# Differences of cumulative sums in a state-space layer: a matmul with split bfloat16 sums in place of a broadcast load

## The chip, the core and the metric

The kernel runs on one core of a Trainium2 chip. Its time is the device time of one execution, in microseconds (us). The core has TensorE (PE in the profile: matmuls; PEld: the loading of their weights), VectorE (DVE), ScalarE (ACT) and GpSimd (POOL). SyncE's queue (SP) issues nearly all DMA transfers here. Each of these takes its instructions strictly in order. SBUF is the on-chip memory, and PSUM is the small memory that TensorE writes; this kernel uses it in tiles of one bank, [128, 512] float32.

## What is computed

One inference step of a two-layer network on 128 context tokens and 1024 latent tokens, 1152 in all, of width 1024. The even layer, where the change is, has a bidirectional state-space scan beside a pooling branch; the odd layer is attention. The scan works in 9 chunks of 128 tokens, with 16 heads in 4 groups. For each chunk and head it needs the decay between every two tokens of the chunk:

```
a = chunk(dt * A)
a_cs = jnp.cumsum(a, axis=2)
seg = a_cs_t[..., :, None] - a_cs_t[..., None, :]
l_mat = jnp.exp(jnp.where(lower, seg, NEG_INF))
cb = jnp.einsum('bclgn,bcsgn->bcgls', Cc, Bc)
y_diag = jnp.einsum('bcgrls,bcsgrp->bclgrp', cb[:, :, :, None] * l_mat, xdt)
```

There is one such scan forward and one backward over the same tokens, each with its own `dt` and `A`. `seg` is a 128 x 128 matrix of differences for each chunk, head and direction. On one side of the diagonal the forward difference is the smaller one, on the other side the backward one, so that the smaller of the two belongs to the direction that is wanted.

## The kernel before, in words

Matrix products run on pairs of float16 numbers, high and low part, as three matmuls each (`mm3`, L330 to L332). The order of PE is the order of the program. The other engines and SP are ordered by a scheduler of the framework that follows buffers, dependences and priorities. Tiles come from pools with a fixed number of buffers; a new tile waits until the last reader of the buffer's former tile is done.

The even layer is one long stage. `ssd_steps` (L741) goes through the four head groups. For a group it first runs seven **storing steps** of one direction's scan (L841 to L851), then nine **output steps** of the other direction (L868 to L911), one chunk each. Between the small matmuls of these steps the generator yields, and `ssd_group` (L710) fills in a measured amount of other matmuls (`F.take`): projections of later blocks, which are large and always ready. So PE alternates between a few scan matmuls, each waiting for what other engines prepare, and a stretch of this fill.

The small matmuls write PSUM tiles with tag `ss`, of which there are four (five late in the stage). In an output step these are `cb` in `prep` (L815), the state's product `st` (L770), the output `yd` (L889) and the carried states' part `yo` (L898). They take the banks in turn.

What the change touches:

- `dt_branch` (L570) computes the cumulative sums on PE: by token (`cs`, L617 to L623) and by head as rows (L641 to L648). Eight DMAs write the rows to DRAM as `csrow` (L650).
- `decay(c)` (L794) prepares the weights of one chunk in a tile `E` of [128, 2, 4, 128] float32 (halves 0 and 1, four heads), of which there are `NE = 5` buffers. It loads the rows of both directions, copied to all 128 partitions, in one 512 KB DMA (L798). Then for each of four heads: ACT adds the token's own sum to half 0 (L801), DVE adds it to half 1 and takes the smaller of both (L802), and ACT writes the `dt` weights over half 1 (L804). ACT's exponential over four heads (L806) and POOL's product of both halves (L807) end it.
- `prep(c)` (L812) multiplies the weights by `cb` on DVE (L825), and ACT and POOL split the result into M, high and low (L510, L511). Four heads' products of M with x make `yd` (L893).
- `decay` is called in three of the seven storing steps (L847) and at the start of six of the nine output steps, for the chunk three ahead (L870), which makes 36 calls; `prep` is called for the chunk two ahead (L872).

In the profile below, psss is any tile of tag `ss`, xs and xshl are the inputs of the state's product, hst, hb and hf the states, o and u the convolution's buffers, whl the projections' weights.

Of the kernel before, what the change touches and what calls it, by code (L numbers as in the profile page):

```python
# [10 lines left out]
F32 = mybir.dt.float32  # L11
F16 = mybir.dt.float16
I32 = mybir.dt.int32
# [19 lines left out]
# even layer: the projections between the scans, by group; the fill (us of the tensor engine) of a group and the  # L33
# shares of it before its first step, per stored state, in either half of an output step, and per context state; the
# steps of the storing scan after which M is prepared
# [9 lines left out]
# odd layer: the fill of the first block of a head's queries, behind the first head's projections; the first block of a  # L45
# window head against the others; the score banks
# [3 lines left out]
NE = 5  # L50
# atanh(z) / z = 1 + s (c0 + c1 s + ...), s = z**2 <= 1/9, to 4e-10
# [20 lines left out]
class Filler:  # L72
    """projections whose matmuls are laid between the attention's and the scans'"""
# [11 lines left out]
    def to_front(self):  # L85
        """the jobs added with front=True from here on come next, behind the one under way"""
        self.pos = 1 if self.begun else 0
# [40 lines left out]
class OutProj:  # L128
    """x_new = x + gate * (g @ w_out), 128 columns of the result at a time; with rby the first half of g is
    scaled by it (per token) on its way out of PSUM"""  # L130
# [21 lines left out]
    def part(self, nb, ps, c0, c1, i):  # L152
        """the i-th k-tile of the order"""
# [6 lines left out]
    def begin(self, n, nb=0):  # L160
        """up to the n-th k-tile of block nb, all chunks of tokens"""
        for i in range(self.k0[nb], n):
            for ps, (c0, c1) in zip(self.pss[nb], CH3):
                self.part(nb, ps, c0, c1, i)
        self.k0[nb] = n
# [20 lines left out]
    def run(self, xres, ssq, chunk_done, chunks, before=None):  # L186
        """the rest; chunk_done(x tiles, first, last token) once a chunk is whole"""
# [34 lines left out]
class Builder:  # L222
# [82 lines left out]
    # ---------------------------------------------------------------- weights  # L305
    def load_w(self, src, nk=KD, n=P, scale=None, rows=None, pool=None):
        """[128, nk, n] fp32 weights -> (hi, lo) fp16 of 64 * w (* a column scale, or one per k-tile)."""
# [19 lines left out]
    def mm3(self, out, ah, al, bh, bl, start, stop):  # L327
        """out (+)= (ah + al).T @ (bh + bl) without the product of the two low parts"""
# [5 lines left out]
    def g_proj(self, src, hs, evac, pre=None):  # L334
        """channel-major projection: evac(psum [128 ch, 384 tok], first, last token); pre: its weights, and the
        chunks that are done"""
# [16 lines left out]
    def tok_proj(self, src, hs, evac):  # L353
        """token-major projection: evac(psum [128 tok, 3, 128 ch], first chunk)"""
# [13 lines left out]
    # ---------------------------------------------------------------- norms  # L368
    def rsqrt(self, out, v, w, pool=None):
        """out = v**-0.5 elementwise for small [128, w] tiles, v > 0: a first guess from the bits, then Newton"""  # L370
# [11 lines left out]
    def rstd_stats(self, ssq, c0, c1, n):  # L382
        """ssq [128, T] (squares summed over the k-tiles) -> diagonal tiles of rstd for tokens c0:c1"""
# [35 lines left out]
    # ---------------------------------------------------------------- ada  # L419
# [13 lines left out]
    def ada(self, blocks, tag, tile, ahead=False):  # L433
        """up to four column blocks (layer, first column, width up to 512) of the modulations, on column tiles of the
        array; mods [128, 24, 2]: shift 0:8, scale 8:16 (+1), gate 16:24 (/64)"""
# [52 lines left out]
    def modulate(self, hs, xs, rb, mods, c0, c1, ks=range(KD)):  # L488
        """h = x * rstd * (1 + scale) + shift as fp16 (hi, lo) for tokens c0:c1"""
# [23 lines left out]
    # ---------------------------------------------------------------- prologue  # L513
    def prologue(self):
        """the first norm, 512 channels at a time, with the first two projections of the even layer"""
# [225 lines left out]
    def ssd_steps(self, g):  # L741
# [126 lines left out]
        for n, c in enumerate(order):  # L868
            if n + 3 < NCH:
                decay(order[n + 3])  # L870
# [773 lines left out]
```

## Time and profile before

| | |
|---|---|
| three runs | 2298.39, 2302.61, 2303.87 us; median 2302.61 us |
| the profiled execution | span 2299.9 us, from its first to its last instruction; no other time is given for it |
| busy PE, PEld | 2025.4 us (88%), 1449.5 us (63%) |
| busy DVE, ACT, POOL | 1658.4 us (72%), 1275.3 us (55%), 1070.7 us (47%) |
| DMA | 283.17 MB, mean 123 GB/s |
| the 36 broadcasts | 512.0 KB each, 4.0 us from issue to landing |

"Busy" counts time in which an instruction runs. PE's matmuls are pipelined, so that one of 384 columns lasts some 0.33 us but the next starts 0.16 us after it. PEclk is the mean clock that TensorE was granted, as a share of full speed. "A <- B" in the list of waits means that A stood idle until B was done.

### The profile page before, as it was taken

The numbers are of one execution on the slowest core, as the hardware profiler recorded it, in microseconds if no ns is written. First come the engines' busy times: TensorE is split into PE (matmuls) and PEld (weight loads), VectorE is DVE, ScalarE is ACT, GpSimd is POOL, SyncE is SP. The second block draws the span as 40 slices with busy tenths as digits, with TensorE's granted clock in tenths as the row PEclk, the third lists the DMA queues.
The fourth block names the chain that finished last, engine by engine and source line by source line (L and its number), as shares of the span: only waits on it lengthen the run. The fifth ranks groups of instructions, "written<-read, shape, count | busy, mean of one in ns | idle before, by whom it ended". The sixth has DMA issues, their size and how long they took to land. (4 is left out here: it accounts for less than half of the span.)

```text
span 2299.9 us, 51010 instructions
## 1 busy us (share of the span) xinstructions
PE 2025.4 (88%) x20258; PEld 1449.5 (63%) x20258; DVE 1658.4 (72%) x3483; ACT 1275.3 (55%) x3432; POOL 1070.7 (47%) x997
## 2 busy tenths in 40 slices
PE   5997788788999999989898898998978898988997
PEld 2654475654657555657586686676666777676566
DVE  5878989789585544768978978878888767663334
ACT  5575656666464211447666666676667756673321
POOL 1378677876774100154534435445446656552001
PEclk9998899998999999999999999999999999999999
DMA  7221514224657412136445455455466867889412
GB/s 283 63 82 53 152 46 122 78 82 132 224 180 209 172 63 85 63 100 121 98 109 123 90 121 121 89 122 110 96 121 137 162 145 152 168 170 206 147 47 83
DMA packets 434990, 283.17 MB, mean 123 GB/s; under 512 B 374432, under 2 KB 385216, under 8 KB 434752
## 3 DMA queue, kind: packets, MB, share of 16 engines
q1 hardware_dynamic: 433776, 279.34, 49.0%
q8 instruction: 158, 2.59, 0.5%
q10 hardware_dynamic: 976, 0.58, 0.1%
q14 instruction: 80, 0.66, 0.1%
HBM read 133.38 MB, written 29.05 MB: 71 GB/s over the span
## 5 line engine op out<-in xcount | busy, mean ns | idle before, releaser
L330 PE MATMUL psmm<-h,whl 128*128 128x384 f16 (+1 forms) x1104 | 366.4, 333 | 9.7 <-DVE V L1205 3.8
L331 PE MATMUL psmm<-h,whl 128*128 128x384 f16 (+1 forms) x1104 | 365.7, 332 | 2.4 <-DVE h L507 1.7
L332 PE MATMUL psmm<-h,whl 128*128 128x384 f16 (+1 forms) x1104 | 365.1, 332 | 0.0
L330 PE MATMUL psmm<-whl,h 128*128 128x128 f16 x1920 | 346.2, 225 | 0.0
L331 PE MATMUL psmm<-whl,h 128*128 128x128 f16 x1920 | 345.8, 224 | 0.0
L332 PE MATMUL psmm<-whl,h 128*128 128x128 f16 x1920 | 345.5, 224 | 0.0
L331 PEld LDWEIGHTS <-whl 128*128 128x128 f16 x2256 | 224.8, 100 | 155.4 <-issue 30.7
L332 PEld LDWEIGHTS <-whl 128*128 128x128 f16 x2256 | 224.4, 99 | 155.1 <-issue 16.0
L330 PEld LDWEIGHTS <-whl 128*128 128x128 f16 x2256 | 225.5, 100 | 149.4 <-issue 21.5
L1307 POOL TENSOR_TENSOR phl<-p,phl 128x1152 f16<-128x1152 f32 (+1 forms) x72 | 158.4, 2200 | 242.4 <-ACT phl L1306 208.7
L324 DVE SCALAR_TENSOR_TENSOR whl<-w,whl 128x512 f16<-128x512 f32 x248 | 211.3, 875 | 67.8 <-ACT whl L323 67.4
L330 PEld LDWEIGHTS <-h 128*128 128x128 f16 x2520 | 251.2, 100 | 9.5 <-issue 3.8
L331 PEld LDWEIGHTS <-h 128*128 128x128 f16 x2520 | 251.1, 100 | 7.6 <-issue 1.9
L332 PEld LDWEIGHTS <-h 128*128 128x128 f16 x2520 | 250.9, 100 | 0.0
L1289 ACT ACTIVATE p<-psS,sms 128x384 f32<-128x384 f32 (+1 forms) x240 | 136.4, 570 | 100.3 <-DVE sms L1286 100.2
L1387 POOL TENSOR_TENSOR phl<-p,phl 128x1024 f16<-128x1024 f32 (+2 forms) x72 | 134.2, 1864 | 120.4 <-ACT phl L1386 120.1
L323 ACT ACTIVATE whl<-w 128x512 f16<-128x512 f32 x248 | 140.0, 609 | 81.3 <-PE psmm L332 44.7
L1173 POOL TENSOR_TENSOR sw<-sw,sin 128x384 f32<-128x384 f32 (+1 forms) x78 | 84.7, 1087 | 147.7 <-DVE sw L1172 134.9
L1280 PEld LDWEIGHTS <-Q 128*128 128x128 f16 x800 | 73.7, 98 | 126.0 <-issue 91.3
L504 POOL TENSOR_TENSOR h<-mt,h 128x384 f16<-128x384 f32 (+2 forms) x32 | 29.3, 925 | 251.6 <-ACT h L503 251.6
L1280 PE MATMUL psS<-K,Q 128*128 128x384 f16 (+1 forms) x480 | 109.5, 323 | 41.6 <-ACT p L1289 41.4
L1303 DVE SCALAR_TENSOR_TENSOR p<-p,sms,p 128x384 f32<-128x384 f32 (+1 forms) x200 | 136.7, 718 | 2.0
(394 smaller groups left out, 6242.5 us busy)
## 6 DMA issues: line engine op xcount, KB each, us to landing
w<-in_wod SPq DMA_DIRECT2D x52, 512.0 KB, 3.7
w<-in_wev SPq DMA_DIRECT2D x40, 512.0 KB, 4.1
E<-csrow SPq DMA_DIRECT2D x36, 512.0 KB, 4.0
Q<-qhl SPq DMA_DIRECT2D x64, 288.0 KB, 4.5
go_dr<-gl SPq DMA_DIRECT2D x15, 576.0 KB, 3.2
wada<-in_w_ada SPq DMA_DIRECT2D x32, 256.0 KB, 5.8
o<-in_w_ada SPq DMA_DIRECT2D x16, 512.0 KB, 5.9
xT<-in_w_ada SPq DMA_DIRECT2D x16, 512.0 KB, 5.9
```

Of the source, the lines that this page charges most:

```text
L323: nc.scalar.activation(hl[:, 0, a:e], w[:, a:e], AF.Copy if scale is None else AF.Identity, scale=sc)
L324: nc.vector.scalar_tensor_tensor(hl[:, 1, a:e], w[:, a:e], sc, hl[:, 0, a:e], ALU.mult, ALU.subtract)
L330: mm(out, ah, bh, start=start, stop=False)
L331: mm(out, ah, bl, start=False, stop=False)
L332: mm(out, al, bh, start=False, stop=stop)
L504: nc.gpsimd.tensor_tensor(h[:, 1, a:b], o, h[:, 0, a:b], ALU.subtract)
L1173: nc.gpsimd.tensor_tensor(sw[:, o:], sw[:, o:], self.sinT[:, a:b], ALU.mult)
L1280: nc.tensor.matmul(sv, q[:, m, x, qs], k[:, m, o + c0:o + c1], start=x == 0, stop=x == 1)
L1289: nc.scalar.activation(pm[:, c0:c1], ss[j], AF.Exp, bias=nb, accum_out=sm[:, i:i + 1])
L1303: nc.vector.scalar_tensor_tensor(p[0][:, c0:c1], p[1][:, c0:c1], sm[:, 2:3], p[0][:, c0:c1], ALU.mult, ALU.add)
L1307: nc.gpsimd.tensor_tensor(phl[:, w:2 * w], p[0][:, :w], phl[:, :w], ALU.subtract)
L1387: nc.gpsimd.tensor_tensor(phl[:, 2 * w:4 * w], p, phl[:, :2 * w], ALU.subtract)
```

## The change

The sums `cs` are no longer added by token on ACT and DVE. Instead PE forms the difference. `dt_branch` splits each row of sums into three bfloat16 parts that add up to it (`part`, one ACT copy each and a DVE subtraction after the first two), and writes all three to DRAM. For each group six small DMAs (`load_csl`) put the parts of four heads and two directions on 24 partitions of a tile `csl`, whose partitions 24 to 26 hold -1. A tile `csr` has two slots; partitions 0 to 23 hold a constant pattern of ones (`pick`), and two small DMAs per chunk (`load_csr`) put the parts of that chunk's sums on partitions 24 to 26. One matmul for each direction then gives the differences of four heads in a whole bank of tag `ss`, with the sign turned round. ACT copies the first bank out, DVE takes the larger of it and the second, and the exponential turns the sign back.

```diff
-NE = 5
+NE = 4
...
+            part = self.tl(self.plp, [P, 2 * TW], BF16, "V", 3)[0:16]
...
-            for g in range(4):
-                nc.sync.dma_start(self.csrow[g, :, d].rearrange("c h l -> h c l"),
-                                  row[g * 4:(g + 1) * 4].rearrange("h (c l) -> h c l", l=P))
+            for i in range(3):
+                h = part[:, (i % 2) * TW:(i % 2) * TW + T]
+                nc.scalar.activation(h, row, AF.Copy)
+                if i < 2:
+                    nc.vector.tensor_tensor(row, row, h, ALU.subtract)
+                nc.sync.dma_start(self.csrow[d, i], h)
+        self.load_csl(0)
+        self.cs_seq = [(g, c) for g in range(4) for c in (range(NCH) if g % 2 == 0 else range(NCH - 1, -1, -1))]
+        self.load_csr(0)
+        self.load_csr(1)
+
+    def load_csl(self, g):
+
+        for d in range(2):
+            for i in range(3):
+                o = 12 * d + 4 * i
+                self.nc.sync.dma_start(self.csl[o:o + 4], self.csrow[d, i, g * 4:(g + 1) * 4])
+
+    def load_csr(self, n):
+
+        if n < len(self.cs_seq):
+            g, c = self.cs_seq[n]
+            for d in range(2):
+                self.nc.sync.dma_start(self.csr[24:27, n % 2, d].rearrange("i (h l) -> i h l", l=P),
+                                       self.csrow[d, :, g * 4:(g + 1) * 4, c * P:(c + 1) * P])
...
         def decay(c):
...
-            nc.sync.dma_start(ef, self.csrow[g, c].rearrange("d h l -> (d h l)").partition_broadcast(P))
+            pd = []
+            for d in range(2):
+                pd.append(self.pt("ss"))
+                nc.tensor.matmul(pd[d], self.csl[:, c * P:(c + 1) * P], self.csr[:, n % 2, d], start=True, stop=True)
+            self.load_csr(n + 2)
+            if g < 3 and n % NCH == NCH - 1:
+                self.load_csl(g + 1)
+            nc.scalar.activation(ef[:, :512], pd[0], AF.Copy)
+            nc.vector.tensor_tensor(ef[:, :512], pd[1], ef[:, :512], ALU.max)
             for hh in range(4):
                 i = g * 4 + hh
-                nc.scalar.activation(E[:, 0, hh], E[:, 0, hh], AF.Identity, bias=self.cs[:, c, i:i + 1])
-                nc.vector.scalar_tensor_tensor(E[:, 0, hh], E[:, 1, hh], self.cs[:, c, 16 + i:17 + i], E[:, 0, hh],
-                                               ALU.add, ALU.min)
                 nc.scalar.activation(E[:, 1, hh], self.tri[:, 0], AF.Identity, bias=self.dt[:, c, 16 + i:17 + i],
                                      scale=self.dtd[:, c, i:i + 1])
-            nc.scalar.activation(E[:, 0], E[:, 0], AF.Exp)
+            nc.scalar.activation(E[:, 0], E[:, 0], AF.Exp, scale=-1.0)
             nc.gpsimd.tensor_tensor(E[:, 0], E[:, 0], E[:, 1], ALU.mult)
...
         for n, c in enumerate(order):
-            if n + 3 < NCH:
-                decay(order[n + 3])
             if n + 2 < NCH:
                 Ms[order[n + 2]] = prep(order[n + 2])
...
                          xk[:, hh // 2, 1, c % 3, hc], True, True)
+            if n + 3 < NCH:
+                decay(order[n + 3])
             nc.vector.tensor_tensor(y[:, c], y[:, c], yd[:, :256], ALU.add)
```

The tile of `cs` is given up and lies in a shared buffer; `even` sets up `csl` and `csr` at its start, with three memsets and two copies on POOL and one load of `pick` on ACT's queue. The call in the output steps is moved behind the matmuls of `yd`.

The orders below show three places. The lines of the changed kernel are some 1 to 56 higher than those before; the numbers behind the names tell buffers and tiles apart.

PE, the first storing step of the first group. Before, behind the last matmul of the first state's product (psss_1390) comes fill at once (psada_1369):

```order
L332 LDWEIGHTS bk_149_1239
L332 MATMUL psss_1390<-xshl_1387,bk_149_1239 128x256
L330 LDWEIGHTS whl_1364
L330 MATMUL psada_1369<-h_309,whl_1364 128x384
L331 LDWEIGHTS whl_1364
L331 MATMUL psada_1369<-h_309,whl_1364 128x384
```

Now (the same product is psss_1419, the same fill psada_1398):

```order
L333 LDWEIGHTS bk_154_1268
L333 MATMUL psss_1419<-xshl_1416,bk_154_1268 128x256
L828 LDWEIGHTS csl_657
L828 MATMUL psss_1425<-csr_658,csl_657 128x512
L828 LDWEIGHTS csl_657
L828 MATMUL psss_1427<-csr_658,csl_657 128x512
L331 LDWEIGHTS whl_1393
L331 MATMUL psada_1398<-h_309,whl_1393 128x384
```

The two matmuls of the first `decay` now stand between the state's product and the fill, and with them what they read: `csl` and `csr`.

SP's queue, the same place. Before, writes of `csrow` (V_1196 and V_1216 are the two directions' rows), two transposing loads (bk), the first three broadcasts to E and a load of weights (w):

```order
L650 DMA csrow<-V_1196 4x9x128
L737 DMA_TRANSPOSE bk_151_1244<-bc_1045 128x6x128
L737 DMA_TRANSPOSE bk_149_1239<-bc_1045 128x6x128
L650 DMA csrow<-V_1196 4x9x128 x2
L650 DMA csrow<-V_1216 4x9x128 x2
L798 DMA E_1395<-csrow 128x1024
L798 DMA E_1515<-csrow 128x1024
L798 DMA E_1664<-csrow 128x1024
L313 DMA w_259_2039<-in_wev 128x1024
```

Now (V_1206 holds the parts of the first direction, V_1231 those of the second), behind the same transposing loads:

```order
L761 DMA_TRANSPOSE bk_156_1273<-bc_1054 128x6x128
L761 DMA_TRANSPOSE bk_154_1268<-bc_1054 128x6x128
L656 DMA csrow<-V_1206 16x1152 x2
L656 DMA csrow<-V_1231 16x1152
L667 DMA csl_657<-csrow 4x1152 x2
L656 DMA csrow<-V_1231 16x1152
L667 DMA csl_657<-csrow 4x1152
L674 DMA csr_658<-csrow 3x4x128
L656 DMA csrow<-V_1231 16x1152
L667 DMA csl_657<-csrow 4x1152
L674 DMA csr_658<-csrow 3x4x128
L314 DMA w_269_2049<-in_wev 128x1024
```

Writes of the parts and reads of what was written alternate in one queue, ahead of the next load of weights; one more read of `csl` and the next reads of `csr` follow behind it.

DVE, an output step of the second group, from the sums into y to the next xs. Before:

```order
L895 TENSOR_TENSOR y_3798<-y_3798,psss_4024 128x256
L904 TENSOR_TENSOR psss_4038<-psss_4038,ef_1182 128x512
L906 TENSOR_TENSOR y_3798<-y_3798,psss_4038 128x256 x2
L802 SCALAR_TENSOR_TENSOR E_4210<-E_4210,cs_1180 128x128 x2
L819 ISA dgs_4088,dgc_4087<-psss_4083,ident 128x128
L819 ISA dgc_4087 128x1
L802 SCALAR_TENSOR_TENSOR E_4210<-E_4210,cs_1180 128x128
L821 SCALAR_TENSOR_TENSOR dgc_4087<-dt_892,dgc_4087,rows 128x4
L825 TENSOR_TENSOR E_3960<-E_3960,psss_4083 128x512
L761 TENSOR_TENSOR x_564_4502<-xk_302_2356 128x256
L767 TENSOR_TENSOR xs_4506<-x_564_4502,dec_1189 128x256
```

Now:

```order
L927 TENSOR_TENSOR y_3821<-y_3821,psss_4030 128x256
L833 TENSOR_TENSOR E_4043<-psss_4046,E_4043 128x512
L936 TENSOR_TENSOR psss_4059<-psss_4059,ef_1191 128x512
L938 TENSOR_TENSOR y_3821<-y_3821,psss_4059 128x256 x2
L851 ISA dgs_4093,dgc_4092<-psss_4088,ident 128x128
L851 ISA dgc_4092 128x1
L857 TENSOR_TENSOR E_4043<-E_4043,psss_4088 128x512
L853 SCALAR_TENSOR_TENSOR dgc_4092<-dt_901,dgc_4092,rows 128x4
L785 TENSOR_TENSOR x_602_4504<-xk_319_2379 128x256
L791 TENSOR_TENSOR xs_4508<-x_602_4504,dec_1198 128x256
```

The four small instructions of L802 are gone, one of 512 elements (L833) stands in their place, and the product with `cb` (L857, before L825) now works on the same tile, E_4043, as L833 just ahead of it; before, E_4210 was prepared while the product worked on E_3960.

More of the change, by code (lines that the diff above doesn't have):

```diff
@@ L12 @@
 F16 = mybir.dt.float16
+BF16 = mybir.dt.bfloat16
 I32 = mybir.dt.int32
@@ L621, in dt_branch @@
                 nc.tensor.matmul(pc[:, o:o + 16], self.tri[:, d], a[:, o:o + 16], start=True, stop=True)
-        cs = t("cs")
+        cs = self.tl(self.plp, [P, TW], F32, "V", 3)[:, :n]
         nc.scalar.activation(cs, pc[:, :n], AF.Copy)
@@ L635, in dt_branch @@
         nc.vector.scalar_tensor_tensor(dec, dec, WS, dt, ALU.mult, ALU.mult)
-        self.dt, self.cs, self.ef, self.etot, self.dec = map(v3, (dt, cs, ef, etot, dec))
+        self.dt, self.ef, self.etot, self.dec = map(v3, (dt, ef, etot, dec))
         self.dtd = self.wt([P, NCH, 16], F32, tag="dtd", bufs=1)
         nc.vector.tensor_tensor(self.dtd, self.dt[:, :, 0:16], self.dt[:, :, 16:32], ALU.subtract)
-        self.csrow = self.dr.tile([4, NCH, 2, 4, P], F32, name="csrow")
+        self.csrow = self.dr.tile([2, 3, 16, T], BF16, name="csrow")
         for d in range(2):
             row = self.tl(self.plp, [P, TW], F32, "V", 3)[0:16, :T]
+            part = self.tl(self.plp, [P, 2 * TW], BF16, "V", 3)[0:16]
             for c0, c1 in CH3:
@@ L794, in decay @@
         def decay(c):
+            n = self.cs_n
+            assert self.cs_seq[n] == (g, c)
+            self.cs_n += 1
             ef = self.wt([P, 1024], F32, tag="E", bufs=NE)
             E = ef.rearrange("p (a b c) -> p a b c", a=2, b=4)
-            nc.sync.dma_start(ef, self.csrow[g, c].rearrange("d h l -> (d h l)").partition_broadcast(P))
+            pd = []
[7 more added lines that the diff above has]
+            nc.vector.tensor_tensor(ef[:, :512], pd[1], ef[:, :512], ALU.max)
             for hh in range(4):
                 i = g * 4 + hh
-                nc.scalar.activation(E[:, 0, hh], E[:, 0, hh], AF.Identity, bias=self.cs[:, c, i:i + 1])
-                nc.vector.scalar_tensor_tensor(E[:, 0, hh], E[:, 1, hh], self.cs[:, c, 16 + i:17 + i], E[:, 0, hh],
-                                               ALU.add, ALU.min)
                 nc.scalar.activation(E[:, 1, hh], self.tri[:, 0], AF.Identity, bias=self.dt[:, c, 16 + i:17 + i],
                                      scale=self.dtd[:, c, i:i + 1])
-            nc.scalar.activation(E[:, 0], E[:, 0], AF.Exp)
+            nc.scalar.activation(E[:, 0], E[:, 0], AF.Exp, scale=-1.0)
             nc.gpsimd.tensor_tensor(E[:, 0], E[:, 0], E[:, 1], ALU.mult)
@@ L1019, in even @@
         with self.scope("ssd"):
+            self.csl = self.wt([P, T], BF16, "csl", 1)
+            self.csr = self.wt([P, 2, 2, 512], BF16, "csr", 1)
+            self.cs_n = 0
+            nc.gpsimd.memset(self.csl, 0.0)
+            nc.gpsimd.memset(self.csr, 0.0)
+            nc.gpsimd.memset(self.csl[0:27], -1.0)
+            pick = self.tl(self.plp, [P, TW], F32, "V", 3)[0:24, :1024].rearrange("p (d a) -> p d a", d=2)
+            nc.scalar.dma_start(pick, A["pick"])
+            for i in range(2):
+                nc.gpsimd.tensor_copy(self.csr[0:24, i], pick)
             for kind, p in zip(("xa", "xb", "b", "c"), (*pre, None, None)):
@@ L1622, in layout @@
     L["rce"] = rce.reshape(-1)
+    pick = np.zeros((2, 3, 4, 2, 4, P), np.float32)
+    for d in range(2):
+        for h in range(4):
+            pick[d, :, h, d, h] = 1.0
+    L["pick"] = pick.reshape(24, 2, 512)
     return {k: np.ascontiguousarray(v) for k, v in L.items()}
```

## Prediction

> **What bounds the kernel now.** I read first the page, for the span of 2299.9 us, and then the table of stretches, because the change touches only the even layer's scans. The first and the last broadcast (L798) start at 131.6 and 671.4 us, so I cut 130 to 708 us into the four groups' storing and output steps. The columns are the stretch and its length, then busy us and count of instructions for PE, PEld, DVE, ACT and POOL, then PEclk, DMA share and GB/s:
>
> ```profile
> 130.00:182.00 52.00, 47.12 (x284) 28.24 (x283) 39.46 (x53) 35.71 (x90) 41.53 (x50) 0.93 0.23 79
> 182.00:277.00 95.00, 68.57 (x499) 42.74 (x498) 84.98 (x142) 56.88 (x137) 72.43 (x87) 0.86 0.33 97
> 277.00:333.00 56.00, 49.97 (x601) 40.20 (x600) 45.35 (x67) 33.03 (x91) 41.15 (x48) 1.00 0.31 92
> 333.00:414.00 81.00, 65.94 (x523) 42.74 (x521) 73.80 (x132) 51.83 (x136) 63.16 (x72) 0.94 0.38 106
> 414.00:475.00 61.00, 49.51 (x566) 38.63 (x563) 47.77 (x67) 39.65 (x115) 52.81 (x84) 0.92 0.18 53
> 475.00:553.00 78.00, 59.35 (x419) 37.05 (x417) 68.62 (x124) 49.52 (x121) 54.93 (x56) 0.88 0.36 101
> 553.00:646.00 93.00, 88.36 (x869) 57.93 (x868) 62.35 (x109) 50.16 (x143) 64.86 (x95) 0.99 0.56 186
> 646.00:708.00 62.00, 57.08 (x454) 32.70 (x453) 50.54 (x111) 34.28 (x79) 37.16 (x46) 0.94 0.60 216
> ```
>
> The rows alternate, storing and output. In the output steps of the first three groups (rows 2, 4 and 6; 254 us) DVE is busy 227.4 us, which is 90%, and PE only 193.9 us, so PE idles 60 of the 92 us that it idles in the whole stage. There DVE is nearly full and PE waits; in the storing steps and in the last group PE is the fuller one. The list of waits of PE in the same 578 us names the releasers (total, times, longest):
>
> ```profile
> PE psss L330 <- ACT xshl L510: 27.3, 6, 10.2
> PE psss L330 <- DVE E L825: 22.9, 10, 4.4
> PE psss L331 <- POOL xshl L511: 19.2, 12, 3.0
> PE psss L330 <- DVE hst L780: 6.7, 6, 2.3
> PE psm L330 <- DVE u L965: 2.6, 1, 2.6
> ```
>
> DVE ends 32.2 us of it in these rows; ACT and POOL, on the way of the state's input xshl, end 46.5 us. The broadcast itself is in none of them: no PE wait ends on a DMA of E. So what counts is what the change takes from DVE and ACT, and what it adds to PE.
>
> **What it removes.** Groups of instructions, 130 to 708 us (count, busy, mean ns, then idle before and its releaser):
>
> ```profile
> L802 DVE SCALAR_TENSOR_TENSOR E<-E,cs 128x128 f32<-128x128 f32 x144 | 72.6, 539 | 6.0 <-ACT E L801 5.9
> L825 DVE TENSOR_TENSOR E<-E,psss 128x512 f32<-128x512 f32 x36 | 24.4, 677 | 0.0
> L804 ACT ACTIVATE E<-tri,dt,dtd 128x128 f32<-128x128 f32 x144 | 66.5, 486 | 42.8 <-DVE E L802 42.3
> L801 ACT ACTIVATE E<-E,cs 128x128 f32<-128x128 f32 x144 | 48.3, 389 | 22.8 <-DMA E<-csrow 22.8
> L806 ACT ACTIVATE E<-E 128x512 f32<-128x512 f32 x36 | 22.1, 616 | 0.0
> ```
>
> 144 DVE instructions of 539 ns, 72.6 us, go. In their place stand 36 of 128 x 512 from PSUM and SBUF, the form of L825: 36 x 0.677 = 24.4 us. DVE is relieved by 48.2 us. ACT loses 48.3 us and gets 36 copies like L806, 22.1 us: relieved by 26 us. The 512 KB loads, 36 of them, go too; no PE wait hangs on them, so I count them at nothing.
>
> L802 by stretch, in the three output rows and for all eight:
>
> ```profile
> 182.00:277.00 95.00, 13.22 (x24) 0.86 0.33 97
> 333.00:414.00 81.00, 13.84 (x24) 0.94 0.38 106
> 475.00:553.00 78.00, 10.37 (x22) 0.88 0.36 101
> ```
>
> In the three DVE-bound stretches 37.4 us leave and 18 x 0.677 = 12.2 us come: 25.2 us net. If these stretches follow DVE, they shrink by 25.2 x 254/227.4 = 28 us; if the waits that DVE ends are only the last links of longer chains, by nothing. By the share of DVE in PE's waits, 32.2/92 = 35%, it would be 10; by DVE's share of being busy, 90%, 25. I take 15, nearer the waits, since they say what came last. **Term 1: -15 us** (-28 to 0).
>
> A wait that ends returns clock as well. In those stretches the clock was 0.86, 0.94 and 0.88, so PE's busy time holds 68.6 x 0.14 + 65.9 x 0.06 + 59.4 x 0.12 = 20.7 us of slow clock. With 15 of 60 us of idle gone, a quarter of it: **term 2: -5 us** (-9 to 0). One wait and the matmuls behind it, beside an undisturbed one:
>
> ```profile
> 156.21 0.37 PE L331 MATMUL psss<-xshl,bk 128*128 128x256 f16 x1 [2.70 <-POOL xshl L511]
> 156.37 0.42 PE L332 MATMUL psss<-xshl,bk 128*128 128x256 f16 x1
> 163.16 0.27 PE L330 MATMUL psss<-xshl,bk 128*128 128x256 f16 x1
> ```
>
> After 2.70 us of idle the same matmul took 0.37 to 0.42 us and not 0.27. The Trainium skill, page "TensorE: Matmul & The Clock Gate", section "What's actually happening", says that the clock falls to half only after at least one idle window of some 3.4 us. By that rule most waits that DVE ends (longest 4.4 us, on average 2.3) cost no clock, term 2 would be about -1, and the sum below 4 us higher; the row shows a slow clock after a shorter wait, and I follow the row.
>
> Third, ACT. L804 overwrites the half that L802 reads, so ACT stood 42.3 us behind DVE, with the state's xshl queued behind it. The new L833 does not read that half; this wait goes, and nothing of DVE takes its place but the exponential, which waits for the maximum. At one place it reaches PE:
>
> ```profile
> 433.12 0.49 ACT L804 ACTIVATE E<-tri,dt,dtd 128x128 f32<-128x128 f32 x1 [3.68 <-DVE E L802]
> 436.42 0.37 PE L330 MATMUL psss<-xshl,bk 128*128 128x256 f16 x1 [6.38 <-ACT xshl L510]
> ```
>
> The largest single wait on xshl, 10.2 us, began with ACT waiting for a load of a state, which the change leaves alone. I take 3.68 for this one and one more us for smaller ones: **term 3: -5 us** (-10 to 0).
>
> **What it adds.** PE gets 72 matmuls of 512 columns. Those of 384 columns start 0.16 us apart:
>
> ```profile
> 130.80 0.33 PE L330 MATMUL psada<-h,whl 128*128 128x384 f16 x1
> 130.96 0.33 PE L331 MATMUL psada<-h,whl 128*128 128x384 f16 x1
> ```
>
> That is 0.16 x 512/384 = 0.215 us each, 15.5 us for all. 36 of them fall into the three stretches where PE idles 60 us; that idle time covers them. The other 36, in the storing steps and the last group, where PE is 81 to 95% busy, lie on the path: **term 4: +8 us** (0 if all are covered, +15.5 if that idle time is not free but sits behind the same chains).
>
> Next, the start. The first `decay` now stands in PE's queue right behind the first state's product, at 130.9 us, and all fill queues behind it. It needs `csl` and `csr`, which come through DRAM:
>
> ```profile
> 130.69 0.27 PE L332 MATMUL psss<-xshl,bk 128*128 128x256 f16 x1
> 128.73 1.66 SPq L650 DMA_DIRECT2D csrow<-V  x4
> 136.06 0.33 SPq L313 DMA_DIRECT2D w<-in_wev  x1
> hst<-in_st SPq DMA_DIRECT2D x8, 128.0 KB, 2.3
> ```
>
> SP comes to this place at 128.7, issues a write in 1.66/4 = 0.42 us, and a small load has landed 2.3 us after its issue. By the new order three writes are followed by reads, of which each waits for its write: the read behind the first write can go at 131.0, then two reads, a write, a read, a `csr`, and the last write at about 133; it lands at 135.4, its read at 138.1. PE stands from 130.9 to 138.1, 7.2 us, and about 1 us more at a slow clock. The wait of 2.70 us at 156 (above) has its causes on POOL, which catches up meanwhile; I take it off. The ten small ACT and DVE instructions that split the rows end before, at some 1.2 us each. The next weights, 136.06 before, go at about the same time. **Term 5: +6 us** (+1 if the queue reaches this place earlier, +12).
>
> Last, PSUM. An output step took four `ss` banks and now takes six, of four there are: each bank must be read after half a step and not a whole one. The reads are L825's 0.68 us on DVE and its like, and PE's cover between two uses is at least the 18 fill matmuls that the order has between a product and the next (2.9 us). **Term 6: +2 us** (0 to +10). The small loads of one chunk wait for the chunk two before, on SP, with weights' loads behind them; I count that at nothing, as whl has three buffers, and as a rival below. `NE = 4` costs nothing, as with the call moved behind `yd` no fifth tile is alive.
>
> **Sum:** -15 - 5 - 5 + 8 + 6 + 2 = -9 us, a span of 2290.9. The median of the runs is 2.7 us above the profiled span, so 2302.6 - 9 = **2293.6 us**. A measurement of this kernel can tell about 0.3%, 6.9 us, from no change.
>
> **The rivals.** *DVE decides all* (0.18): the three stretches shrink in step with DVE, terms 1 to 3 at their ends but for a little (-28, -9, -7), costs as above: -28 us, 2274.6. For it: DVE's 90%. Against it: the waits that ACT and POOL end.
>
> *Nothing freed counts* (0.10): PE's waits run through POOL, whose work the change leaves, so terms 1 to 3 are nothing: +16, 2318.6. For it:
>
> ```profile
> DVE xs L767 <- POOL xshl L511: 36.8, 22, 5.8
> L807 POOL TENSOR_TENSOR E<-E 128x512 f32<-128x512 f32 x36 | 51.7, 1439 | 17.3 <-ACT E L806 17.2
> ```
>
> *The weights come too late* (0.13), the rival on the other side: a chunk's weights are now begun at the end of one output step and used by DVE's product at the start of the next. Copy (0.6), maximum (0.68), exponential (0.62) and POOL's product (1.44) make 3.3 us; PE covers it with `yo` (six matmuls of 256 columns, 0.66) and 18 of fill (2.9), 3.6 us. If queues on ACT and POOL make the chain longer, DVE, in order, stands in front of L857, with x and xs behind it, and each us more than 0.3 is lost 24 times. It decides from about 1.3 us: then 24 us of DVE eat the 25 won. At 1.8 us term 1 becomes +9 and term 2 nothing: +20, 2322.6. Before, the product never waited (idle before L825: 0.0), because the weights had a whole step.
>
> *SP eats it* (0.09): SP's queue holds weights behind a small load that waits for PE, some 2 us at five places: +10 on the forecast, about 2303.
>
> That the broadcast stays in some form is excluded by the order: no L798 is left.
>
> **How the numbers follow.** The forecast has 0.50, with its own range of -20 to +3 us. Of that I count 0.32 as faster by over 0.3%, 0.15 within, 0.03 slower; the first rival is faster, the second and third slower, the last within for 0.07. Faster 0.50, same 0.22, slower 0.28. The range goes from the first rival with all terms at their ends, 2268, to the second, 2318.
>
> **What would show it.** In the profile after: DVE busy in the stage down by some 48 us, ACT's wait behind L802 gone, the PE waits that end on DVE's products down by a third or more, 72 matmuls 0.21 us apart, and a wait of some 7 us before the first of them. Wrong would be: an idle time before the product with `cb` (the chain is late), PE waits of the new matmuls on banks, or PE waits on weights after small loads. If DVE falls by 48 us and PE idles as long as before, term 1 is wrong.

## The result, and the profile after

| | before | after |
|---|---|---|
| median (4 runs each) | 2303.2 us | 2322.6 us |
| ratio, 95% interval | | 1.0080 (1.0068 to 1.0093) |
| span of the profiled execution | 2299.9 us | 2322.6 us |
| busy DVE, ACT, PE | 1658.4, 1275.3, 2025.4 us | 1626.8, 1259.3, 2043.2 us |

The change made the kernel slower by 0.8%, some 18 us. Work did go from DVE and ACT, and PE's own work grew. In all, DVE's busy time fell by 31.6 us, less than the 48 us that leave the decays: the splits of the rows add 7.3 us, and some other groups take longer. The even layer's stage ends 24 us later (last `yd` at 730.8 us and not 706.7); behind it both kernels take the same time (1591.8 and 1593.2 us).

The stretches of the changed kernel that answer to the three output windows and to the last group's output, cut at about the same matmuls (columns as before):

```profile
196.00:289.00 93.00, 71.38 (x511) 43.93 (x510) 75.29 (x122) 48.91 (x107) 70.04 (x81) 0.89 0.21 55
343.00:433.00 90.00, 68.42 (x489) 42.03 (x489) 75.16 (x120) 49.80 (x123) 74.72 (x95) 0.85 0.23 49
484.00:566.00 82.00, 60.59 (x423) 36.69 (x421) 68.99 (x109) 48.12 (x109) 55.29 (x56) 0.90 0.20 54
666.00:732.00 66.00, 61.49 (x485) 34.32 (x478) 45.85 (x95) 32.78 (x69) 34.45 (x42) 0.97 0.45 155
```

DVE is no longer nearly full in the first three: 219.4 of 265 us, 83%, where it was 90%. Yet they are longer (265 and not 254 us), and PE idles 64.6 us in them, where it idled 60. So PE now waits with DVE less busy. The list of PE's waits, from 95 to 735 us, says for what:

```profile
PE psss L331 <- DVE hst L804: 36.3, 17, 4.6
PE psss L332 <- POOL xshl L512: 11.0, 5, 5.0
PE psss L828 <- ACT bc L703: 7.5, 1, 7.5
PE psss L331 <- ACT xshl L511: 6.2, 2, 4.1
PE psss L828 <- DVE hst L804: 6.1, 2, 5.1
PE psss L828 <- DVE y L938: 5.9, 4, 2.2
PE psss L331 <- DMA bk<-bc: 5.9, 1, 5.9
PE psss L828 <- DVE E L857: 4.8, 6, 1.5
```

The waits on the state's input xshl shrank, from 27.3 (ACT) and 19.2 (POOL) to 6.2 and 11.0 us, and those on DVE's weights (22.9) went. In their place stand 36.3 us for L804, before L780, which had 6.7. L804 is the instruction with which DVE reads the state's product `st` out of its bank. Of the 17 matmuls that wait for it 16 are those of `yo` (L331 with hb or hf), which do not use that result at this point: they want the bank.

One such place, first before the change, from PE's and DVE's timelines (start, duration):

```profile
640.29 0.27 PE L332 MATMUL psss<-xshl,bk 128*128 128x256 f16 x1
...
640.77 0.28 PE L330 MATMUL psss<-hb,bc 128*128 128x256 f16 x1
...
645.80 0.41 DVE L780 SCALAR_TENSOR_TENSOR hst<-psss,hst 128x256 f32<-128x256 f32 x1
```

and the same place in the changed kernel:

```profile
653.85 0.27 PE L333 MATMUL psss<-xshl,bk 128*128 128x256 f16 x1
...
655.52 0.59 PE L828 MATMUL psss<-csr,csl 128*128 128x512 bf16 x1 [1.05 <-DVE hst L804]
656.33 0.59 PE L828 MATMUL psss<-csr,csl 128*128 128x512 bf16 x1 [0.22 <-DVE E L857]
661.00 0.39 PE L331 MATMUL psss<-hb,bc 128*128 128x256 f16 x1 [4.08 <-DVE hst L804]
...
660.53 0.41 DVE L804 SCALAR_TENSOR_TENSOR hst<-psss,hst 128x256 f32<-128x256 f32 x1
```

In both kernels DVE reads the product late, 5.5 us after it in the first and 6.7 us in the second; until then its timeline is full of other instructions. Before, nobody minded; `yo` began 0.5 us after the product. Now the bank that `yo` gets is the product's, and PE stands 4.08 us until DVE has read it. Why it is that bank: there are four, taken in turn. Before, a step took `cb`, `st`, `yd`, `yo`, and `yo` got the bank of the former step's `yo`. Now it takes `cb`, `st`, `yd`, D, D, `yo` (D for the two matmuls of L828). Four back from `yo` is `st` of the same step, with no fill between the two on PE.

### The profile page after: what moved, and what is told of

Read it like the earlier page. It is cut to its first block, busy times and chain, and to the rows that moved or that the text cites. A ratio compares the mean times of both kernels' runs of the same rounds, so it can differ in the third digit from the quotient of the medians.

```text
span 2322.6 us, 50967 instructions
## 1 busy us (share of the span) xinstructions
PE 2043.2 (88%) x20330; PEld 1457.2 (63%) x20330; DVE 1626.8 (70%) x3379; ACT 1259.3 (54%) x3330; POOL 1084.3 (47%) x1002
## 5 line engine op out<-in xcount | busy, mean ns | idle before, releaser
L331 PE MATMUL psmm<-h,whl 128*128 128x384 f16 (+1 forms) x1104 | 364.4, 331 | 7.7 <-DVE V L1248 3.8
L331 PE MATMUL psmm<-whl,h 128*128 128x128 f16 x1920 | 346.5, 225 | 0.0
L331 PEld LDWEIGHTS <-whl 128*128 128x128 f16 x2256 | 225.1, 100 | 150.8 <-issue 21.8
L325 DVE SCALAR_TENSOR_TENSOR whl<-w,whl 128x512 f16<-128x512 f32 (+1 forms) x248 | 206.0, 854 | 77.5 <-ACT whl L324 77.2
L331 PEld LDWEIGHTS <-h 128*128 128x128 f16 x2520 | 251.6, 100 | 10.0 <-issue 3.8
```

The costliest lines, as they stand in the source:

```text
L325: nc.vector.scalar_tensor_tensor(hl[:, 1, a:e], w[:, a:e], sc, hl[:, 0, a:e], ALU.mult, ALU.subtract)
L331: mm(out, ah, bh, start=start, stop=False)
```

## The experiments

The theory that the above suggests: **the banks**, with PE's time for the new matmuls. Its rivals: the **weights too late** of the prediction, and the **start**, where the traces show 21 us lost at once. Ratios are against the kernel before, run on the same chip.

**The call first again.**

```diff
+            if n + 3 < NCH:
+                decay(order[n + 3])
             if n + 2 < NCH:
                 Ms[order[n + 2]] = prep(order[n + 2])
...
-            if n + 3 < NCH:
-                decay(order[n + 3])
```

> Changed kernel with decay called at the start of an output step again (NE stays 4). Bank theory: in the changed kernel the six ss tiles of a step stand in the order cb, st, yd, D, D, yo over four banks, so that yo takes the bank of the state's product st of the same step, which DVE (L804) has only just to read; 36.3 us of PE waits end on that line. With the call in front the order is D, D, cb, st, yd, yo: yo takes the bank of the second D, read half a step before. Then the waits on L804 fall below 10 us, the three output windows lose some 20 us, and the time is about 2303 us (2297 to 2308). Weights-too-late theory (the rival on record): what is lost is DVE waiting at the product with cb for the weights (idle before L857 8.6 us in the changed kernel); that goes, for at most 9 us: about 2314. Start theory: the 24 us at the end of the stage are the 21 us lost at the first decay, and moving the call changes nothing: 2320 or more.

Measured: 2312.1 us, ratio 1.0043 (1.0028 to 1.0057). Half of the expected 20 us came. PE's waits in that kernel:

```profile
PE psss L828 <- DVE hst L804: 18.0, 10, 5.4
PE psss L331 <- DVE y L927: 14.0, 4, 7.4
PE psss L331 <- DVE E L833: 10.0, 9, 2.0
```

The wait on L804 left `yo` and went to the D matmuls: with the order D, D, `cb`, `st`, `yd`, `yo` the second D gets the bank of the former step's `st`. A fill of half a step lies between, and DVE is at times later than that. `cb` and `yd` now wait for DVE's other reads. The bank theory said where the waits were, not that six tiles on four banks always have such a place.

**A fifth bank for the scans in three groups.**

```diff
-            self.banks["mm"] = ["mm", "mm", "m3", "ada"]
+            self.banks["mm"] = ["mm", "mm", "m3"]
+            self.banks["ss"] = ["ss"] * 4 + ["ada"]
...
                     F.side, F.every = side(), ADA_EVERY
+                    self.banks["ss"] = ["ss"]
```

> Changed kernel with a fifth bank for ss in the first three groups, taken from the fill (three banks left to it); the call stays behind yd. With five banks yo takes the bank of cb of the same step, read before the fill in the middle of the step. Bank theory: the waits on L804 fall below 10 us in the first three groups, as with the call in front, and the time falls by 10 to 18 us (2305 to 2313), less what the fill loses with three banks (up to 5 us). Weights-too-late theory: no gain, since the chain of the weights is as it was: 2318 to 2330. Start theory: no gain either.

Measured: 2312.2 us, 1.0041 (1.0027 to 1.0056): 9 to 10 us under the changed kernel, with the call where the change put it. The weights-too-late theory said no gain. The waits on L804, 36.3 and 6.1 us in the changed kernel, fell to 7.8 and 6.4 us:

```profile
PE psss L828 <- DVE y L938: 9.7, 3, 5.8
...
PE psss L331 <- DVE hst L804: 7.8, 6, 4.3
...
PE psss L828 <- DVE hst L804: 6.4, 2, 5.5
```

So 28 us of waits went and 9 to 10 us of time: a wait that is taken away is in good part replaced by another one.

**Both together.** The two edits above in one kernel.

> Changed kernel, nothing left out, with both remedies: five ss banks in the first three groups and decay called at the start of the output step. If both took away the same loss, PE waiting for a bank that DVE has still to read (10.5 us each): 2307 to 2313, the call's earlier place being worth at most the 5.6 us that moving it cost the kernel before. If the call first was worth its 10.5 us for another reason (weights ready half a step earlier): both add up, 2299 to 2304. Waits of PE on the reading of the state's product (36.3 us in the changed kernel, 18.0 and 4.9 us with the call first, 7.8 and 6.4 us with five banks) fall below 10 us in any case.

Measured: 2309.7 us, 1.0032 (1.0019 to 1.0045). The two do not add up, as the bank theory said. That they take away the same loss is not shown by it, since the waits on L804 did not fall below 10 us as I had said. They are 21.7 us, 8 of the 11 before a matmul of `cb`: with six tiles on five banks and this order, `cb` gets the bank of the former step's `st`.

**The first decay later.**

```diff
-DECAY_AT, PREP_AT = (0, 2, 4), (5, 6)
+DECAY_AT, PREP_AT = (1, 3, 5), (5, 6)
```

> Changed kernel with decay in the second, fourth and sixth storing steps and not the first, third and fifth: the first decay's matmuls come 5.5 us of fill later, so that in the first group PE reaches them after the rows have landed (the last small read was issued at 146.6 us and PE stood until 149.7). Start theory: the wait of 7.5 us goes and stays gone: 2312 to 2316. Bank theory: the delay of 21.3 us against the kernel before shrank to 5.7 us by the first output step anyway, since the kernel before loses there in other ways, so at most 5 us of the time go: 2317 to 2323.

Measured: 2320.5 us, 1.0074 (1.0060 to 1.0088). The start theory falls: the second state's product came 11.4 us after that of the kernel before and not 21.3, and the time is within the noise of the changed kernel's (1.0080).

**The relief alone.** In the kernel before:

```diff
+            nc.scalar.activation(ef[:, :512], ef[:, :512], AF.Copy)
+            nc.vector.tensor_tensor(ef[:, :512], ef[:, 512:], ef[:, :512], ALU.min)
             for hh in range(4):
                 i = g * 4 + hh
-                nc.scalar.activation(E[:, 0, hh], E[:, 0, hh], AF.Identity, bias=self.cs[:, c, i:i + 1])
-                nc.vector.scalar_tensor_tensor(E[:, 0, hh], E[:, 1, hh], self.cs[:, c, 16 + i:17 + i], E[:, 0, hh],
-                                               ALU.add, ALU.min)
```

> Kernel before, with its broadcast, but the four ACT additions of a decay replaced by one ACT copy of 512 columns and the four DVE operations by one minimum of 512 columns: the work of ACT and DVE per decay of the changed kernel, without its matmuls, banks, small loads or moved call. It leaves out the addition of the token's own sums. The prediction's terms 1 to 3 by themselves: -25 us, about 2278 (2256 to 2303). If nothing freed counts, because PE's waits run through POOL: 2300 to 2306. If DVE decides all: about 2260.

Measured: 2291.8 us, 0.9945 (0.9929 to 0.9961). Terms 1 to 3 are worth 11 to 13 us and not 25. The relief of DVE is smaller here than in the changed kernel, since the minimum takes 1.0 us on average:

```profile
L800 DVE TENSOR_TENSOR E<-E 128x512 f32<-128x512 f32 x36 | 36.1, 1004 | 11.1 <-ACT E L799 11.1
L767 DVE TENSOR_TENSOR xs<-x,dec 128x256 f32<-128x256 f32 x64 | 45.0, 712 | 51.7 <-POOL xshl L511 42.7 <-DMA out_ssd<-xs 4.5 <-POOL x L761 4.3
```

**The moved call alone**, in the kernel before (the diff of the first experiment the other way round, with five buffers of E).

> Kernel before with one thing of the change alone: decay(n+3) is called behind the matmuls of yd and not at the start of the output step (NE stays 5, the broadcast stays). Bank theory: its decay takes no bank, so the moved call costs nothing: 2298 to 2308. Weights-too-late theory: a chunk's weights have half a step less before DVE's product needs them, and the broadcast and the eight small operations are a longer chain than the changed kernel's: slower by 10 to 25 us, with an idle time before the product with cb (L825).

Measured: 2309.5 us, 1.0024 (1.0012 to 1.0035), 5.5 us slower. Neither expectation holds: it costs something, but DVE never waited at the product (idle before L825 0.0 us). In its trace L802's instructions took 604 ns on average and not 539 (82.1 us busy and not 72.6), and PE waited once 7.9 us for one of them. Why they took longer, and whether the 5.5 us lie there, is open.

**No matmuls in three groups.** The D matmuls of the first decay write a bank of their own, which all later decays of these groups read; the fill keeps three banks.

```diff
+            if g < 3:
+                if n == 0:
+                    self.pdx = self.pt("ada")
+                    for d in range(2):
+                        nc.tensor.matmul(self.pdx, self.csl[:, c * P:(c + 1) * P], self.csr[:, n % 2, d], start=True, stop=True)
+                pd = [self.pdx, self.pdx]
...
```

> Changed kernel in which the decays of the first three groups have no matmuls but the first two: ACT's copy and DVE's maximum read one bank that is written once (taken from the fill, which keeps three), so no ss bank is taken either. It leaves out the differences of those chunks, and its exponential has a small scale there. Splits, small loads, start and the call behind yd are as in the changed kernel, and so is the fourth group. If matmuls and banks make up what separates the changed kernel (2322.6) from the relief alone (2291.8): 2297 to 2303, the start's few us on top of 2291.8 and a third of the fourth group's loss. If the remaining loss is in the splits, the small loads or the start: 2308 or more.

Measured: 2304.2 us, 0.9999 (0.9989 to 1.0009).

**The matmuls in a bank of their own.** As that, with `if True:` in place of `if n == 0:`.

> As the kernel without matmuls, but with them: both matmuls of each decay go, one over the other, to the one bank outside ss, which ACT's copy and DVE's maximum read (it leaves out the first direction's differences, and the exponential has a small scale in the first three groups). Against the kernel without matmuls the difference is PE's time for 54 matmuls, 54 x 0.215 = 11.6 us if all of them lie on the path, 4 us by the prediction's term 4; against the changed kernel it is what the coupling through the ss banks costs. Bank theory: 8 to 14 us under the changed kernel, 2309 to 2315, near the kernel with five banks. If PE idles for other reasons behind the same chains, both differences are under 4 us.

Measured: 2312.6 us, 1.0041 (1.0027 to 1.0055). The kernel without matmuls still has two of the 54, so the difference is that of 52. They cost 0.42%, 9.7 us, of the 52 x 0.215 = 11.2 us that they take, and the shared banks of these groups 0.39%, 9.0 us: as much as the fifth bank gave back. By the intervals, each of these two differences can be off by some 4 us.

**No matmuls at all.** As the kernel without matmuls in three groups, and in the fourth the copy and the maximum read a constant in SBUF.

> As the kernel without matmuls in the first three groups (2304.2), but in the fourth group too the copy and the maximum read a constant (from SBUF, in which the maximum takes longer, 1.0 us in the relief alone, as against 0.68 us from PSUM), so that no decay has matmuls or takes a bank of ss; it leaves out all differences, and the exponential has a small scale throughout. Splits, small loads, the wait at the start, the call behind yd and three banks for the fill are as they were. If matmuls and banks are the whole loss: the fourth group no longer loses the 11 us that it lost in the trace, and the time is that of the relief alone, 2288 to 2295. If start, splits, small loads or the moved call keep a cost of their own: 2297 to 2304.

Measured: 2292.7 us, 0.9955 (0.9942 to 0.9969): the time of the relief alone. This kernel has the splits, the small loads, the moved call and the whole start:

```profile
PE psada L830 <- DMA csl<-csrow: 8.1, 1, 8.1
```

So these together cost little that lasts. That they cost nothing is not shown. The two ratios leave room for some 5 us either way. In 27 of its 36 decays the maximum reads PSUM and takes 0.68 us, so DVE is relieved by some 8 us more than in the relief alone, and the broadcasts are gone; that may hide a cost, such as the 5.5 us of the moved call. The run also shows that the fourth group's matmuls and banks cost 0.44%, 10 us. The traces, one execution of each kernel, agree. The table has the start of the same matmul in each kernel less its start in the kernel before, in us, from PE's timelines:

```
matmul (start before)            changed  call   own   none in  none    relief
                                          first  bank  3 groups at all  alone
first state's product  (130.47)    10.9   10.1    8.9     9.2     7.0     1.6
second                 (136.16)    21.3   20.4   19.2    20.0    18.4     1.6
ninth                  (196.68)     5.7    7.6    3.2    10.2     8.1    -1.4
last yd, first group   (274.15)    12.0    3.2    4.2     7.5     6.9    -4.6
last yd, second group  (411.70)    20.5   10.8   12.5     3.6     1.8    -1.4
last yd, third group   (565.77)    13.0   11.9    5.0    -8.5    -8.6   -13.9
fourth group, output   (640.07)    11.9   14.3    4.2    -9.5    -9.2    -8.4
last yd of all         (706.74)    24.1   19.2   14.9     1.7    -7.5    -7.9
```

Read the first two rows, then the third: 20 us lost at the start are 3 to 10 by the ninth product, because the kernel before has its longest wait there (10.2 us, on xshl), which a later PE does not meet. Read the last two: whoever has D matmuls in the fourth group loses 5 to 12 us in it, who has none, 0 to 2.

**The start eased, and no splits.** On top of the call first and the later first decay, the writes of `csrow` go on ACT's queue; then, in a further kernel, each row is copied once and written three times.

```diff
-                nc.sync.dma_start(self.csrow[d, i], h)
+                nc.scalar.dma_start(self.csrow[d, i], h)
```

> Changed kernel, nothing left out, with the call of decay at the start of the output step (2312.1 by itself), the first decay one storing step later (2320.5 by itself, 2.1 under the changed kernel), and the writes of csrow on ACT's queue, right behind the copies that make them, so that ACT no longer waits 8.3 us for a write that stands behind the transposing loads in SP's queue. If the start's delay lasts (in the kernel without matmuls PE stood 10 us behind the kernel before at the first output step, against -1 us in the relief alone): 2303 to 2307. If it is caught up, as with the later first decay alone: 2308 to 2312.

> As the kernel with the call first and the start eased, but each row of sums is copied to bfloat16 once and that copy is written three times: four subtractions on DVE (7 us) and four copies on ACT (5 us) ahead of the first bk loads are left out, and with them the exactness of the sums. If the splitting delays the first state's product (10.9 us behind the kernel before in the changed kernel) and this lasts: 3 to 8 us under the former. If not: within 2 us of it.

Measured: 2317.0 us, 1.0073 (1.0059 to 1.0087), and 2313.0 us, 1.0048 (1.0036 to 1.0061). The first is slower than the call first alone, which neither theory said; in the traces both end their stage alike (19.1 and 19.2 us behind). These two do not tell the theories apart, and why the eased start costs time is open.

**Other ways to relieve.** Both start from the kernel before and leave nothing out. One minimum on DVE, all additions on ACT:

```diff
                 nc.scalar.activation(E[:, 0, hh], E[:, 0, hh], AF.Identity, bias=self.cs[:, c, i:i + 1])
-                nc.vector.scalar_tensor_tensor(E[:, 0, hh], E[:, 1, hh], self.cs[:, c, 16 + i:17 + i], E[:, 0, hh],
-                                               ALU.add, ALU.min)
+                nc.scalar.activation(E[:, 1, hh], E[:, 1, hh], AF.Identity, bias=self.cs[:, c, 16 + i:17 + i])
+            nc.vector.tensor_tensor(ef[:, :512], ef[:, 512:], ef[:, :512], ALU.min)
+            for hh in range(4):
+                i = g * 4 + hh
```

> Kernel before, broadcast and all, and nothing left out: ACT adds the tokens' own sums to both halves (eight additions and not four), and DVE takes one minimum of 512 columns (0.68 us) in place of four operations (2.16 us). DVE is relieved by some 50 us as in the changed kernel, ACT is loaded with 56 us more and not relieved. If DVE's relief is what counted in the relief alone (2291.8): 2292 to 2298. If it was ACT's, or if ACT becomes the bound, with longer waits on xshl from ACT: 2303 to 2320.

Measured: 2305.2 us, 1.0008 (0.9996 to 1.0019). And the first direction's sum in the exponential:

```diff
+        nc.vector.tensor_tensor(self.cs[:, :, 16:32], self.cs[:, :, 16:32], self.cs[:, :, 0:16], ALU.subtract)
...
-                nc.scalar.activation(E[:, 0, hh], E[:, 0, hh], AF.Identity, bias=self.cs[:, c, i:i + 1])
...
+                nc.scalar.activation(E[:, 0, hh], E[:, 0, hh], AF.Exp, bias=self.cs[:, c, i:i + 1])
...
-            nc.scalar.activation(E[:, 0], E[:, 0], AF.Exp)
```

> Kernel before, broadcast and all, nothing left out, with another way to relieve ACT: the own sum of the first direction is taken out of the minimum and added as the bias of the exponential, which becomes four instructions of 128 columns and not one of 512; the second direction's own sum is replaced once by the difference of both. ACT's four additions go (48.3 us) and the exponential costs 26 us more; DVE's work stays and no longer waits for ACT. With one minimum on DVE and ACT loaded nothing was won (2305.2), with both relieved 10.7 us. If ACT's relief is the part that counts: 2294 to 2299. If both are needed, or DVE alone decides: 2300 to 2304.

Measured: 2309.7 us, 1.0035 (1.0021 to 1.0048), slower though ACT does less; why is open. Neither of these two ways won anything. What DVE's relief is worth without a load on ACT they do not tell, as the first puts 56 us of additions on ACT. No version that computes everything beat the kernel before.

## Why the prediction was wrong

It said 2293.6 us (2268 to 2318), faster; it is 2322.6, slower. As shares of some 2303 us, four measured steps lead from the kernel before to the changed one: everything but the matmuls and their banks (no matmuls at all), -10 us; the fourth group's matmuls and banks, +10; the matmuls of the other three groups, +9.7; their shared banks, +9.0. That these come to +18 proves nothing, since each step starts where the one before it ended; what the runs show is how the loss divides, each part to within some 4 us. (The fill has a fourth bank only in the kernel before and the changed one, so the shared banks may cost a little more.) Put in the prediction's terms, the relief is worth -10 (-13 by the relief alone), the matmuls cost +13 (9.7 for 52, 3.4 for the fourth group's 18) and the banks +16, of which 9.0 are measured and 6.7 are an estimate, what is left of the fourth group's 10.1 without its matmuls.

Two steps failed by about as much: the banks by 14 us, and the relief (terms 1 to 3 together) by 12 to 15. With only one of them right the sum would have come out some 4 us above the kernel before. Only the banks cost more than the bounds that the prediction gave.

- **Term 6, the banks (+2, at most +10): the step that failed.** They cost about +16. The prediction said that "PE's cover between two uses is at least the 18 fill matmuls that the order has between a product and the next". That holds between a step's products, not between `st` and `yo`, which have the twelve small matmuls of `yd` and the two D between them. The order showed it; I counted banks per step (six on four) and not which tile gets whose bank. And I priced the read by its duration (0.68 us) and not by how late DVE comes to it (5.5 to 6.7 us above).
- **Term 1, DVE's relief (-15):** In the decays DVE was relieved as said, by 48.1 us: L802's 72.6 us became these 24.5:

```profile
L833 DVE TENSOR_TENSOR E<-psss,E 128x512 f32<-128x512 f32 x36 | 24.5, 681 | 4.5 <-ACT E L832 4.5
L791 DVE TENSOR_TENSOR xs<-x,dec 128x256 f32<-128x256 f32 x64 | 45.3, 717 | 58.8 <-POOL xshl L512 48.5 <-DMA out_ssd<-xs 7.7 <-POOL x L785 2.2
```

  Part of it became idle time behind POOL, which is next in the chain of a state. Before the change the same group of DVE had

```profile
L767 DVE TENSOR_TENSOR xs<-x,dec 128x256 f32<-128x256 f32 x64 | 47.9, 758 | 45.4 <-POOL xshl L511 39.3 <-DMA out_ssd<-xs 3.7 <-POOL x L761 2.1
```

  39.3 us behind POOL, and now 48.5. The rival "nothing freed counts" was half right: terms 1 to 3 together are -10 to -13 and not -25. I also took busy time for work. L802's 144 instructions took 0.336 us at the least and 0.342 at the median, but up to 2.315 us; at the median they would be 144 x 0.342 = 49 us, so that at least some 23 of the 72.6 us are instructions drawn out. L833, with an operand in PSUM, was never drawn out (0.673 to 0.692 us). How much of the missing gain this explains no run tells.
- **Term 2, the clock (-5):** none came back; it was 0.86, 0.94 and 0.88 in the three windows and is 0.89, 0.85 and 0.90, and PE waits no less (64.6 us idle, before 60).
- **Term 3, ACT (-5):** ACT's 42.3 us behind L802 are gone, and 8.8 us of the exponential behind L833 are left. But the prediction said that "nothing of DVE takes its place but the exponential", and something did: ACT's part of the split of M waits for the product with `cb`, first before the change, then after:

```profile
L510 ACT ACTIVATE E<-E 128x512 f16<-128x512 f32 x36 | 22.3, 620 | 9.3 <-DVE E L825 4.5 <-POOL E L807 2.1 <-POOL x L761 1.6
L511 ACT ACTIVATE E<-E 128x512 f16<-128x512 f32 x36 | 22.5, 625 | 38.4 <-DVE E L857 38.3
```

  So at these places ACT waits for DVE as long as before: 42.3 and 4.5 us, now 8.8 and 38.3. PE's waits on xshl fell by 29 us all the same; why is not shown. What the term is worth by itself no run tells.
- **Term 4, the matmuls (+8):** 0.22 us apart as said. The idle time of PE hides few of them: 9.7 of 11.2 us came, to within some 4 us, and not half.
- **Term 5, the start (+6):** larger at its place (21 us by the second product) and little or nothing at the end. Three rows of SP, ACT and PE show a loop that I did not see:

```profile
135.31 4.48 SPq L761 DMA_TRANSPOSE bk<-bc  x2
...
142.69 1.16 ACT L653 ACTIVATE V<-V 16x1152 bf16<-16x1152 f32 x1 [8.28 <-DMA csrow<-V]
...
141.38 0.40 PE L331 MATMUL psss<-xshl,bk 128*128 128x256 f16 x1 [5.86 <-DMA bk<-bc]
149.71 1.01 PE L828 MATMUL psss<-csr,csl 128*128 128x512 bf16 x2 [7.50 <-ACT bc L703]
```

  The third part of a row reuses the first one's half of a buffer. Its copy on ACT waits 8.28 us for the first part's write, which stands in SP's queue behind the transposing loads; those wait for POOL's part of bc, which comes later than before. PE then waits twice. The releaser named last, a copy to bc, has nothing to do with D; in the kernel without matmuls the same wait is put down to the load of `csl`.
- **The rivals.** *The weights come too late* gave 2322.6, the time measured, but that is a coincidence: DVE waited 8.6 us before L857 and not 1.8 us in each of 24 steps. The lateness shows on ACT, in the 38.3 us above; in the kernel without any matmuls ACT still waits 20.5 us for this product, and the loss is gone. *SP eats it*: SP stood 81.9 us in 24 waits of L674 for PE, and no wait of PE in the stage was for whl. *DVE decides all* is excluded by the relief alone.
- **The sums.** Two figures do not follow from their terms. At 1.8 us the third rival loses 1.5 x 24 = 36 us against 25 won, which makes term 1 +11 and not +9, and its time 2324.6. The lower end with all terms at their ends is -28 - 9 - 10 + 0 + 1 + 0 = -46 us, 2256.6 and not 2268. And the upper end, 2318, left out the third rival's 2322.6, and costs at their own upper bounds with nothing won (15.5, 12 and 10 us) would be 2340.

## What to carry to other kernels

When a change adds tiles to a ring of PSUM banks, write out for each tile whose bank it takes, and look what stands on PE between the two; price the wait by how late the reading engine is in its own queue, not by how long the read takes. Before counting an instruction's busy time as work that can be saved, look at its shortest and median time beside the mean. What an engine's relief is worth can be tried by itself, by leaving the work out, before anything is put in its place. A large loss at the start of a stage need not last: follow the same matmul through both traces to its end.

## What the runs showed of the hardware

- A maximum or minimum of 128 x 512 float32 took 0.67 to 0.69 us on DVE with one operand in PSUM, in all 36 of the changed kernel. With both operands in SBUF the shortest took the same 0.68 us, but the mean was 1.00 us and the longest 2.85 in the relief alone, and 0.83 us on average with one minimum on DVE. The longer ones ran beside POOL's instructions for half of their time or more; that POOL draws them out is not tested by a run.
- One wait does not tell the clock of what follows. I had read a clock loss from a wait of 2.70 us in the kernel before, after which the matmul took 0.37 us. In the same trace one of 3.39 us, at 352.14 us, left it at 0.27 us, and so did this one of 2.46 us:

```profile
321.02 0.27 PE L331 MATMUL psss<-xshl,bk 128*128 128x256 f16 x1 [2.46 <-POOL xshl L511]
```

  By the rule of the Trainium skill, page "TensorE: Matmul & The Clock Gate", section "What's actually happening", that the clock falls after at least one idle window of some 3.4 us, none of these waits would have slowed PE. The waits of 2.46 and 3.39 us fit that; the one of 2.70 us does not, and there the measurement decides. What makes the difference is open.
